# Chunk products of a gated DeltaNet: the triangle mask as a third product in the exponent, beta on ScalarE

## The chip, the cores and the metric

The kernel runs on one core of a Trainium2 chip. The metric is device time in microseconds (us) of one execution, the median of the runs shown. The engines are TensorE (PE in profiles; its weight loads are PEld), VectorE (DVE), ScalarE (ACT), GpSimd (POOL) and SyncE (SP), which issues the transfers. Each works through its own queue in order.

## What is computed

One layer over 2048 latent tokens of width 1024 with 256 context tokens: a neighbourhood attention branch and a bidirectional gated DeltaNet branch, both fed by one projection, merged with gates. The change is in the DeltaNet branch, in the part that is done for every chunk of 64 tokens, head and direction before the scan:

```python
gc = jnp.cumsum(g, axis=-1)
decay = jnp.exp(jnp.where(incl, gc[..., :, None] - gc[..., None, :], -jnp.inf))
kb = k * beta[..., None]
lower = jnp.where(strict, jnp.einsum('bnhid,bnhjd->bnhij', kb, k) * decay, 0.0)
a_mat = lower + jnp.eye(C, dtype=f32)
sol = lax.linalg.triangular_solve(a_mat, rhs, left_side=True, lower=True, unit_diagonal=True)
qk = jnp.einsum('bnhid,bnhjd->bnhij', q, k) * decay
```

C is 64; 36 chunks, 8 heads and 2 directions are computed (the context's chunks without the queries).

## The kernel before

The kernel is one program of stages whose instructions overlap: modulation and normalised, transposed inputs; DeltaNet's k and q with convolution; the chunk products (the stage of the change); DeltaNet's v; the attention's projections and bias tables; then scan and attention together, and the output projections. The program is written in stages, and a scheduler at build time puts each engine's instructions into one fixed order from a timeline that it computes. A change of one stage's instructions so moves others' places too. On the chip each engine takes that order as it stands and waits where an operand isn't there.

The stage of the change is the loop over 18 tiles of two chunks (128 tokens) in `kk_tile`. For a tile, the keys and queries `kq` of both chunks are loaded, and TensorE forms k k^T and q k^T for 8 heads in 32 x 64 pieces (L623) into the accumulator `kk`, which has one buffer. Then, for each of two directions d:

- GpSimd multiplies the log decays, split into a high and a low part (`ghi`, `glo`), with the triangle mask `sm`, 128x512 each (L630, tiles `gmh` and `gml`).
- TensorE adds both up with a triangle of ones, `cmr`, into the accumulator `ps` (pool `pe`, two buffers; L633), which gives the sums of log decays between any two tokens.
- ScalarE takes Exp into E (L635, two buffers).
- GpSimd multiplies E with minus beta (L638) and with the mask (L639).
- VectorE multiplies E with the key products into X (L641) and with the query products in place (L643), both 128x512.
- SP stores X to `d_X` and E to `d_A` (L646, L648). A buffer of E is free for a later Exp when its store has landed.

Between the tiles stands other work, by hand in the program: `pump(fill, ...)` takes 47 gate units, each a product group of 24 products 128x512 (L179) that ScalarE evacuates with Tanh (L205) from one of three accumulators `pd` and SP stores (tile `zt`), with weights that are loaded, cast by ScalarE (L124, tile `slots`) and reduced by GpSimd to their low part (L125). From the third tile on, `solve_for(9000)` hands out steps of the triangular solve by a credit in ns. The solve works on VectorE alone: five blocks (tile `Xs`, one buffer, loaded from `d_X` when the tiles that it holds are stored), each of 62 steps, and step m is two instructions over m x (63 - m) columns, a product (L577) and a sum (L579):

```python
V.tensor_tensor(out=tv, in0=X[r, piv, cols].unsqueeze(1).to_broadcast([8 * n, m, w]),
                in1=X[r, rows, piv].unsqueeze(2).to_broadcast([8 * n, m, w]), op=ALU.mult)
V.tensor_tensor(out=X[r, rows, cols], in0=X[r, rows, cols], in1=tv, op=ALU.add)
```

The first block has 64 rows, the others 128. The solve goes on through the stages behind the loop, where other work on VectorE stands between its steps, and ends before the scan begins. L590 copies the first block's reversed half for its store.

## Time and profile before

| what | us |
|---|---|
| runs, median of 3 | 2428.86 |
| runs, lowest and highest | 2428.39, 2434.27 |
| the profiled execution, its own time | 2437.24 |
| its span | 2435.5 |
| loop over the tiles (first L630 to last L643) | 462.2 to 802.6 |
| first and last step of the solve (L577) | 504.7 to 1408.8 |

A profile shows one execution. Busy time of an engine is the time in which it works on an instruction; a wait is put down to what ended it. Lines L... are those of the kernel before. The chain of work that ended last is followed back from the last instruction, at each step to what released it, and says which work set the end. The granted clock is the share of TensorE's full clock in a stretch.

### The profile page before, as it was taken

What the parts mean: (1) busy time and instruction counts of PE and PEld (TensorE: products, weight loads), DVE (VectorE), ACT (ScalarE), POOL (GpSimd) and SP (SyncE); (2) the same over time, 40 slices, a digit from 0 to 9 for tenths busy, and PEclk for the clock granted to TensorE, in tenths of its full rate; (3) what the DMA queues carried; (4) which work ended last, traced back from release to release, by engine and by line L of the source; (5) the groups of instructions that cost most, each with busy time, mean ns of one, the idle gap of its engine ahead of it and who ended that gap; (6) DMA issues with size and microseconds to landing.
All of it is one profiled execution on the core that took longest, in us unless ns stands there. A gap on an engine that the chain in (4) does not pass through costs nothing.

```text
span 2435.5 us, 47134 instructions
## 1 busy us (share of the span) xinstructions
PE 2208.8 (91%) x18323; PEld 1849.1 (76%) x18323; DVE 1537.0 (63%) x2409; ACT 779.9 (32%) x2336; POOL 1064.2 (44%) x856
## 2 busy tenths in 40 slices
PE   6999999988888998998889987989888989899999
PEld 2778777876676787998888766777666767788998
DVE  3736877379959987849849922666566766222222
ACT  4524344211111232343554111444334444211110
POOL 2515677779865211224857510211123324643442
PEclk8999999998998999999999998999999999999999
DMA  7323444665475244254686567777886786544442
GB/s 262 106 70 81 114 118 130 156 152 121 122 173 134 64 88 115 64 131 119 181 200 176 171 153 205 211 195 196 211 216 178 184 195 177 155 118 121 113 115 89
DMA packets 461591, 358.16 MB, mean 147 GB/s; under 512 B 203253, under 2 KB 386697, under 8 KB 460809
## 3 DMA queue, kind: packets, MB, share of 16 engines
q1 hardware_dynamic: 461368, 355.16, 54.7%
q8 instruction: 144, 2.36, 0.4%
q14 instruction: 79, 0.65, 0.1%
HBM read 231.71 MB, written 119.67 MB: 144 GB/s over the span
## 4 chain that ended last, share of the span: by engine, by line
PE 44%; DVE 20%; DMA 12%; POOL 8%; issue 6%; ACT 4%; SPq 3%; DVEq 0%; POOLq 0%; ACTq 0%
PE pd L179 13%; PE pf L1351 7%; PE pu L1340 7%; DVE Xs L579 6%; DVE tmp L577 6%; PE pd L724 5%; PE pw L1063 2%; DMA tedge<-d_tab 2%; ACT pr L1085 2%; PE pc L866 1%; DMA tmk<-in_k_mk_dram 1%; POOL rn L504 1%; PE po L1116 1%; PE pt L1096 1%; DMA d_tab<-tmk 1%
## 5 line engine op out<-in xcount | busy, mean ns | idle before, releaser
L179 PE MATMUL pd<-hT,slots 128*128 128x512 f32 (+1 forms) x3360 | 825.6, 400 | 4.3 <-ACT nx L205 2.5
L179 PEld LDWEIGHTS pd<-hT,slots 128*128 128x128 f32 x3360 | 627.6, 194 | 152.6 <-issue 3.8
L577 DVE TENSOR_TENSOR tmp<-Xs 128x236 f32<-128x236 f32 (+43 forms) x310 | 337.4, 1088 | 62.4 <-DMA Xs<-d_X 54.1
L579 DVE TENSOR_TENSOR Xs<-Xs,tmp 128x236 f32<-128x236 f32 (+43 forms) x310 | 335.8, 1083 | 8.5
L125 POOL TENSOR_TENSOR slots<-w_raw,slots 128x512 fp32r<-128x512 f32 (+1 forms) x76 | 121.0, 1592 | 252.0 <-ACT slots L124 250.2
L724 PE MATMUL pd<-slots,hT 128*128 128x256 f32 x1248 | 165.5, 293 | 0.0
L724 PE MATMUL pd<-wide,hT 128*128 128x256 f32 x1248 | 158.8, 289 | 3.8 <-ACT wide L124 2.6
L724 PEld LDWEIGHTS pd<-slots,hT 128*128 128x128 f32 x1248 | 159.9, 196 | 0.0
L724 PEld LDWEIGHTS pd<-wide,hT 128*128 128x128 f32 x1248 | 155.7, 195 | 4.5 <-ACT wide L124 3.0
L878 POOL TENSOR_TENSOR sd<-sd,gts 128x512 f32<-128x512 f32 x36 | 37.6, 1045 | 238.4 <-PE pc L866 205.6
L1085 ACT ACTIVATE pr<-pr,nm 128x288 f32<-128x288 f32 (+3 forms) x128 | 77.9, 609 | 165.4 <-DVE nm L1082 165.4
L1341 DVE SCALAR_TENSOR_TENSOR gt<-gt,pu 128x256 f32<-128x256 f32 x120 | 46.3, 418 | 122.2 <-DMA gt<-d_g 76.4
L481 DVE SCALAR_TENSOR_TENSOR y<-raw,vT,y 128x512 f32<-128x512 f32 (+1 forms) x112 | 97.0, 875 | 27.5 <-ACT raw L469 22.0
L777 POOL TENSOR_TENSOR tmk<-trr,tmk 128x288 f32<-128x288 f32 (+3 forms) x72 | 98.7, 1387 | 31.0 <-DMA tmk<-in_k_mk_dram 17.3
L1342 POOL TENSOR_TENSOR gt<-gt 128x256 f32<-128x256 f32 x60 | 44.3, 739 | 127.4 <-DVE gt L1341 126.1
L1355 DVE SCALAR_TENSOR_TENSOR ckd<-pf,gate 128x512 f32<-128x512 f32 x32 | 22.0, 692 | 122.1 <-PE pf L1351 115.3
L689 POOL TENSOR_TENSOR nrn<-nss,nhalf 128x8 f32<-128x8 f32 x34 | 74.0, 2177 | 56.8 <-DVE nss L688 55.1
L205 ACT ACTIVATE zt<-pd 128x512 f32<-128x512 f32 x68 | 40.6, 597 | 180.5 <-PE pd L179 113.2
L1340 PE MATMUL pu<-ckq,OS 128*128 128x256 f32 x512 | 95.2, 284 | 2.1 <-DVE gt L1341 1.3
L124 ACT CAST slots<-w_raw 128x512 fp32r<-128x512 f32 (+1 forms) x76 | 46.6, 613 | 151.1 <-DMA w_raw<-in_w_in_dram 120.2
L866 PE MATMUL pc<-sd,ckq 64*64 64x64 f32 x2176 | 85.0, 232 | 8.5 <-DMA ckq<-d_kq 8.3
L866 PEld LDWEIGHTS pc<-sd,ckq 64*64 64x64 f32 x2176 | 75.0, 144 | 22.3 <-issue 11.3
(295 smaller groups left out, 4589.9 us busy)
## 6 DMA issues: line engine op xcount, KB each, us to landing
w_raw<-in_w_in_dram SPq DMA_DIRECT2D x92, 256.0 KB
ckq<-d_kq SPq DMA_DIRECT2D x64, 256.0 KB
gt<-d_g SPq DMA_DIRECT2D x60, 256.0 KB
d_X<-X SPq DMA_DIRECT2D x72, 128.0 KB
Xs<-d_X SPq DMA_DIRECT2D x18, 512.0 KB
d_g<-zt SPq DMA_DIRECT2D x36, 256.0 KB
cv<-d_v SPq DMA_DIRECT2D x72, 128.0 KB
cT<-d_T SPq DMA_DIRECT2D x72, 128.0 KB
```

Of the source, the lines that this page charges most:

```text
L125: G.tensor_tensor(out=lo[:, j:j + 4, 0:n], in0=wr, in1=hi[:, j:j + 4, 0:n].bitcast(F32), op=ALU.subtract)
L179: PE.matmul(ps[0:n, 0:m], a[:, k, 0:n], h_part(g, z, k), start=k == 0 and i == 0, stop=k == KB - 1 and i == 2)
L481: V.scalar_tensor_tensor(out=y[:, 0:m], in0=raw[:, o + j - 1:o + j - 1 + m], scalar=tap(j), in1=y[:, 0:m], op0=ALU.mult, op1=ALU.add)
L577: V.tensor_tensor(out=tv, in0=X[r, piv, cols].unsqueeze(1).to_broadcast([8 * n, m, w]), in1=X[r, rows, piv].unsqueeze(2).to_broadcast([8 * ...
L579: V.tensor_tensor(out=X[r, rows, cols], in0=X[r, rows, cols], in1=tv, op=ALU.add)
L689: G.tensor_tensor(out=rn, in0=ss, in1=nhalf, op=ALU.pow)
L724: PE.matmul(ps[:, 256 * i:256 * i + 256], h[:, 256 * j + P * i:256 * j + P * i + P], w[:, :, part, k, :], start=k == 0 and n == 0, stop=k ...
L777: G.tensor_tensor(out=mv, in0=rr[:, k0:k0 + nr, w0:w0 + n], in1=mv, op=ALU.add)
L866: PE.matmul(ps[half[d], h, :], ld["ckq"][half[d], ho(h), z, :], sd[half[d], h, :], start=True, stop=True)
L1085: S.activation(e[:, 0:nk], e[:, 0:nk], AF.Exp, bias=nm[:, u:u + 1], accum_out=self.sums[:, hh, 0:1])
L1340: PE.matmul(ps, a, r[:, k, :], start=k == 0 and n == 0, stop=k == 3 and n == 2)
L1351: PE.matmul(ps, a[:, k, P * i:P * i + P], b[k, n], start=k == 0 and m == 0, stop=k == KB - 1 and m == 2)
```

## The change

The triangle mask is taken off E and put into the exponent: `smn` holds -1e30 on the diagonal of each chunk (the product of both directions' masks) and 0 elsewhere. Multiplied with the other direction's triangle `cmr[:, 1 - d]` it gives -1e30 to each pair that is to be masked, so that Exp makes 0 of it. This is a third product per direction on TensorE, first of the three. The product with minus beta moves from GpSimd to ScalarE, as eight instructions 128x64 with a scale per partition. GpSimd keeps the two masked decays, now under one name with three buffers. X had one buffer and keeps it.

```diff
--- before.py
+++ after.py
@@ -340,6 +340,9 @@
     cmr = gp.tile([P, 2, P], F32R, name="cmr")
     sm = gp.tile([P, 2, C], F32, name="sm")
     SP.dma_start(out=sm, in_=k_sm)
+
+    smn = gp.tile([P, C], F32R, name="smn")
+    V.scalar_tensor_tensor(out=smn, in0=sm[:, 0], scalar=BIG, in1=sm[:, 1], op0=ALU.mult, op1=ALU.mult)
     edc = gp.tile([P, 2, NTILE, H], F32, name="edc")
     nbeta = gp.tile([P, 2, NTILE, H], F32, name="nbeta")
     ghi = gp.tile([P, 2, NTILE, H], F32R, name="ghi")
@@ -606,6 +609,8 @@
         pk = st.enter_context(tc.tile_pool(reuse_waits="tile", name="pk", bufs=1, space=PSUM))
         pe = st.enter_context(tc.tile_pool(reuse_waits="tile", name="pe", bufs=2, space=PSUM))
 
+        ho = lambda h: h % 4 * 2 + h // 4
+
         def kk_tile(t):
             main = t >= CT
             n = 2 if main else 1
@@ -625,19 +630,19 @@
                 ps = pe.tile([P, H, C], F32, name="pe")
                 gms = []
                 for nm, g in (("gmh", ghi), ("gml", glo)):
-                    gm = kp.tile([P, 2, 4, C], F32R, name=nm)
+                    gm = kp.tile([P, 2, 4, C], F32R, name="gm", bufs=3)
                     gv = g[:, d, t].bitcast(F32).rearrange("p (q u) -> p u q", u=2).unsqueeze(3).to_broadcast([P, 2, 4, C])
                     G.tensor_tensor(out=gm, in0=gv, in1=sm[:, d].unsqueeze(1).unsqueeze(1).to_broadcast([P, 2, 4, C]), op=ALU.mult)
                     gms.append(gm)
+                PE.matmul(ps, cmr[:, 1 - d, :], smn.unsqueeze(1).to_broadcast([P, H, C]), start=True, stop=False)
                 for i, gm in enumerate(gms):
-                    PE.matmul(ps, cmr[:, d, :], gm.rearrange("p u q e -> p (u q) e"), start=i == 0, stop=i == 1)
+                    PE.matmul(ps, cmr[:, d, :], gm.rearrange("p u q e -> p (u q) e"), start=False, stop=i == 1)
                 E = kp.tile([P, H, C], F32, name="E", bufs=2)
                 S.activation(E, ps, AF.Exp)
-                nb = nbeta[:, d, t].rearrange("p (q u) -> p u q", u=2).unsqueeze(3).to_broadcast([P, 2, 4, C])
+                for h in range(H):
+                    S.mul(E[:, h], E[:, h], nbeta[:, d, t, ho(h):ho(h) + 1])
                 a4 = lambda z: z.rearrange("p (u q) e -> p u q e", u=2)
-                G.tensor_tensor(out=a4(E), in0=a4(E), in1=nb, op=ALU.mult)
-                G.tensor_tensor(out=E, in0=E, in1=sm[:, d].unsqueeze(1).to_broadcast([P, H, C]), op=ALU.mult)
-                X = kp.tile([P, H, C], F32, name="X")
+                X = kp.tile([P, H, C], F32, name="X", bufs=1)
                 V.tensor_tensor(out=a4(X)[:, :, :, ::-1] if d and not main else a4(X), in0=kk[:, :, :, 0:C], in1=a4(E), op=ALU.mult)
                 if main:
                     V.tensor_tensor(out=a4(E), in0=kk[:, :, :, C:2 * C], in1=a4(E), op=ALU.mult)
```

How the new order stands against the old: on GpSimd 72 instructions fewer (L638, L639), on ScalarE 288 more, on TensorE 36 more, on SP as many as before. By the last X of the loop the solve has done 93 steps where it had done 89; the gate products in the loop are 837 where they were 835, counted from the first key product to the last product of decays.

GpSimd in the middle of the loop, before (gmh and gml are the masked decays, slots the weights' low part):

```order
L639 TENSOR_TENSOR E<-E,sm 128x512
L630 TENSOR_TENSOR gml<-glo,sm 128x512
L638 TENSOR_TENSOR E<-E,nbeta 128x512
L639 TENSOR_TENSOR E<-E,sm 128x512
L630 TENSOR_TENSOR gmh<-ghi,sm 128x512
L630 TENSOR_TENSOR gml<-glo,sm 128x512
L125 TENSOR_TENSOR slots<-w_raw,slots 128x512
L638 TENSOR_TENSOR E<-E,nbeta 128x512
```

and in the changed kernel, whose lines stand five to six lower (L635 is the old L630):

```order
L635 TENSOR_TENSOR gm<-ghi,sm 128x512
L635 TENSOR_TENSOR gm<-glo,sm 128x512
L635 TENSOR_TENSOR gm<-ghi,sm 128x512
L635 TENSOR_TENSOR gm<-glo,sm 128x512
L125 TENSOR_TENSOR slots<-w_raw,slots 128x512
L635 TENSOR_TENSOR gm<-ghi,sm 128x512
L635 TENSOR_TENSOR gm<-glo,sm 128x512
```

Only decays and weights are left, and no instruction there waits for ScalarE's Exp any more.

TensorE around the key products of the eighth tile, before:

```order
L633 MATMUL pe<-gmh,cmr 128x512
L179 MATMUL pd<-hT_755,slots 128x512 x2
L179 MATMUL pd<-hT_756,slots 128x512
L623 MATMUL kk<-kq 64x128 x16
L633 MATMUL pe<-gml,cmr 128x512
L179 MATMUL pd<-hT_755,slots 128x512 x2
```

and now (L628 is the old L623; L637 the mask's product; L639 the decays'):

```order
L637 MATMUL pe<-smn,cmr 128x512
L639 MATMUL pe<-gm,cmr 128x512 x2
L179 MATMUL pd<-hT_591,slots 128x512 x2
L179 MATMUL pd<-hT_592,slots 128x512
L179 MATMUL pd<-hT_591,slots 128x512
L628 MATMUL kk<-kq 64x128 x16
L637 MATMUL pe<-smn,cmr 128x512
L639 MATMUL pe<-gm,cmr 128x512 x2
```

The two decay products of a direction, which stood apart with gate products between them in many tiles, now mostly follow each other behind the mask's product.

ScalarE around the seventh tile, before (L635 is Exp, L205 a gate evacuation, L124 a weight cast):

```order
L635 ACTIVATE E<-pe 128x512
L124 CAST slots<-w_raw 128x512
L635 ACTIVATE E<-pe 128x512
L205 ACTIVATE zt<-pd 128x512 x2
L635 ACTIVATE E<-pe 128x512
```

and now (L641 is Exp, L643 the eight products with minus beta):

```order
L641 ACTIVATE E<-pe 128x512
L643 ACTIVATE E<-E,nbeta 128x64 x8
L124 CAST slots<-w_raw 128x512
L641 ACTIVATE E<-pe 128x512
L205 ACTIVATE zt<-pd 128x512
L643 ACTIVATE E<-E,nbeta 128x64 x8
L124 CAST slots<-w_raw 128x512
```

Behind the second Exp an evacuation stands ahead of the eight products. That is so in 8 of the 36 directions; in one a weight cast stands there.

## Rows read from the trace of the kernel before

**Rows 1.** Page, part 1: busy us (share of the span) x instructions of each engine.

```profile
PE 2208.8 (91%) x18323; PEld 1849.1 (76%) x18323; DVE 1537.0 (63%) x2409; ACT 779.9 (32%) x2336; POOL 1064.2 (44%) x856
```

**Rows 2.** Stretches: us, busy of PE, PEld, DVE, ACT, POOL, granted clock, DMA share, GB/s.

```profile
462.00:505.00 43.00, 43.00 (x265) 34.24 (x265) 8.58 (x14) 9.65 (x16) 32.25 (x30) 1.00 0.68 152
505.00:700.00 195.00, 159.70 (x885) 124.58 (x885) 188.30 (x170) 29.75 (x51) 161.49 (x94) 0.91 0.53 126
700.00:735.00 35.00, 30.10 (x155) 23.60 (x151) 10.71 (x20) 4.51 (x8) 18.87 (x17) 0.94 0.93 219
735.00:805.00 70.00, 62.70 (x317) 49.37 (x318) 68.83 (x61) 10.92 (x19) 40.56 (x24) 0.89 0.46 111
805.00:900.00 95.00, 91.62 (x464) 76.10 (x463) 92.84 (x120) 37.43 (x73) 16.09 (x8) 0.98 0.23 64
...
1300.00:1410.00 110.00, 106.19 (x468) 85.40 (x467) 106.53 (x90) 23.00 (x63) 65.57 (x40) 1.00 0.54 161
```

**Rows 3.** Chain that ended last, by line: of 505 to 700, then 1300 to 1410 us.

```profile
by line: DVE Xs L579 27.3%; DVE tmp L577 26.7%; issue 17.3%; PE pd L179 9.9%; DVE E L643 4.6%; DMA d_X<-X 4.1%; DVE X L641 2.1%; PE kk L623 1.7%; DMA w_raw<-in_w_in_dram 1.4%; PE pe L633 1.1%; POOL gmh L630 0.8%; DVE zt L207 0.7%; SPq L646 
...
by line: DVE Xs L579 49.0%; DVE tmp L577 47.0%; SPq L586 2.4%; issue 2.3%; DVE nss L688 1.3%; DVE Xs L581 0.1%
```

**Rows 4.** Stretches, VectorE's L577 alone (two rows), then L579 alone (two rows).

```profile
505.00:700.00 195.00, 81.19 (x61) 0.91 0.53 126
...
735.00:805.00 70.00, 31.17 (x24) 0.89 0.46 111
...
505.00:700.00 195.00, 82.33 (x62) 0.91 0.53 126
...
735.00:805.00 70.00, 30.89 (x24) 0.89 0.46 111
```

**Rows 5.** Groups by form, VectorE, 805 to 1000 us: busy us, mean ns, idle before.

```profile
L577 DVE TENSOR_TENSOR tmp<-Xs 128x980 f32<-128x980 f32 x3 | 3.5, 1179 | 0.1
...
L577 DVE TENSOR_TENSOR tmp<-Xs 128x62 f32<-128x62 f32 x2 | 0.5, 244 | 8.5 <-DMA Xs<-d_X 8.5
```

**Rows 6.** Timeline, VectorE and GpSimd at 617 us: start us, us, instruction.

```profile
617.40 1.91 DVE L579 TENSOR_TENSOR Xs<-Xs,tmp 64x980 f32<-64x980 f32 x1
...
618.24 2.22 POOL L639 TENSOR_TENSOR E<-E,sm 128x512 f32<-128x512 f32 x1
```

**Rows 7.** Lines L630 and L641: duration ns min/median/max, first and last start.

```profile
L630 POOL TENSOR_TENSOR gmh<-ghi,sm x36: 1042/1618/1997, 462.2 to 785.1; 128x512 fp32r<-128x512 f32 x36
...
L641 DVE TENSOR_TENSOR X<-kk,E x36: 671/678/693, 476.4 to 800.9; 128x512 f32<-128x512 f32 x36
```

**Rows 8.** Waits from 505 to 700 us: total us, times, longest.

```profile
ACT zt L205 <- PE pd L179: 53.1, 10, 9.2
...
PE pe L633 <- POOL gmh L630: 17.3, 5, 4.5
...
PE pe L633 <- POOL gml L630: 11.2, 3, 4.3
```

**Rows 9.** Groups, GpSimd, 505 to 700 us: busy us, mean ns, idle before.

```profile
L639 POOL TENSOR_TENSOR E<-E,sm 128x512 f32<-128x512 f32 x20 | 38.9, 1946 | 0.7
...
L638 POOL TENSOR_TENSOR E<-E,nbeta 128x512 f32<-128x512 f32 x21 | 33.9, 1612 | 28.2 <-ACT E L635 28.1
```

**Rows 10.** Timeline, VectorE around 700 to 735 us; idle before, and its releaser, in brackets.

```profile
702.22 0.69 DVE L641 TENSOR_TENSOR X<-kk,E 128x512 f32<-128x512 f32 x1 [3.18 <-POOL E L639]
...
710.20 0.69 DVE L641 TENSOR_TENSOR X<-kk,E 128x512 f32<-128x512 f32 x1 [1.84 <-POOL gmh L630]
...
731.11 0.22 DVE L577 TENSOR_TENSOR tmp<-Xs 128x62 f32<-128x62 f32 x1 [11.66 <-DMA Xs<-d_X]
```

**Rows 11.** Chain that ended last, 455 to 475 us, in order of time: start us, us.

```profile
460.59 9.32 PE pd L179 x40
```

**Rows 12.** Chain, 1230 to 1260 us; then groups of ScalarE over the whole span.

```profile
1248.35 1.75 ACT nx L692 x8
...
L692 ACT ACTIVATE nx<-pd,nrn 128x64 f32<-128x64 f32 x224 | 49.1, 330 | 61.3 <-POOL nrn L689 61.1
```

## The prediction

> **What bounds the kernel now.** The page first: of the span of 2435.5 us TensorE is busy 2208.8, VectorE 1537.0, GpSimd 1064.2 and ScalarE 779.9 [rows 1]. Such shares are means over stages, so the table of stretches comes next [rows 2]. The loop over chunk tiles runs from 462 to about 805 us. Up to 505 us TensorE has no gap at all (43.00 of 43.00). From 505 to 700 us three engines crowd: VectorE 188.30 of 195 us, GpSimd 161.49, and TensorE 159.70 at a granted clock of 0.91, a mean between its levels of 1.2 and 2.4 GHz. From 700 to 735 us VectorE has little to do (10.71), and from 735 to 805 us it is full again (68.83 of 70). The chain of work that ended last, asked for by stretch, says who sets the time: from 505 to 700 us the two lines of the solve, L577 and L579, hold 54%; from 1300 to 1410 us they hold 96% [rows 3]. So the time of the loop is read from VectorE.
>
> Why is VectorE full? From 505 to 700 us it runs nearly all of the first solve block: 61 instructions at L577 and 62 at L579, 81.19 + 82.33 = 163.5 us [rows 4]. The same instructions where GpSimd is nearly idle (805 to 900 us, GpSimd 16.09 of 95 [rows 2]) take 1179 ns for 980 columns and 244 ns for 62 [rows 5]: a line of 181 + 1.019 x columns ns. A block has 62 steps, step m with m x (63 - m) columns, 41,664 in all, and two instructions per step: 2 x (62 x 0.181 + 41,664 x 0.001019) = 107.4 us alone. The excess is 163.5 - 107.4 = 56 us. It goes with GpSimd: at 617 us a step of 980 columns takes 1.91 us and GpSimd's L639 beside it 2.22 [rows 6]; GpSimd's own mask product at L630 is 1.04 us at its least and 1.6 in the middle, while VectorE's product with PSUM, L641, stays between 671 and 693 ns [rows 7]. So an instruction of VectorE with both inputs in SBUF and one of GpSimd slow each other. TensorE, for its part, waits for GpSimd's masked decays at L633, 17.3 + 11.2 = 28.5 us in this stretch [rows 8].
>
> **What the change does, and its prices.**
> 1. It removes L638 and L639, the two products on E: 21 + 20 [rows 9] of GpSimd's 94 instructions of the stretch [rows 2], 36 + 36 in the loop. If the excess of 56 us is shared alike by the 94, these take 41/94 x 56 = 24.4 us with them. Bounds: the 53 that stay can hold VectorE for their own 1.04 us each at most, 55 us, so that only 1 us goes; and at the other end all 56 go. I take the share, since shapes and engine stay the same. **-24.4 us**, on the path, as VectorE sets the end there.
> 2. From 735 to 805 us the solve has 24 + 24 instructions in 31.17 + 30.89 = 62.1 us [rows 4]: steps 6 to 29 of the second block, 17,960 columns, alone 2 x (24 x 0.181 + 17,960 x 0.001019) = 45.3 us by the same line. GpSimd has 24 instructions there [rows 2], some 12 of them the removed kinds (two of each four in the loop). Half of 16.8: **-8.4 us** (between 0 and 16.8).
> 3. From 700 to 735 us VectorE waits twice behind GpSimd, 3.18 us for L639 and 1.84 us behind a masked decay; after these it waits 11.66 us for the load of the next solve block [rows 10]. That transfer is late next. **-3 us** of the 5 (0 to 5).
> 4. It adds 36 products of the mask, 128x512 like those of L179 and L633. 40 of L179 took 9.32 us back to back, 0.233 each [rows 11]: 8.4 us in all. About 8 stand in the first stretch, where TensorE has no gap: 8 x 0.233 = **+1.9 us**. The others fall into the 28.5 us of waiting above; if that cover were gone, the other 28 would cost 6.5 us. A mask product stands first of its three and so waits for the Exp two directions before, which frees the accumulator; behind it on TensorE's queue stand the products of L179. Before, the first decay product had the same wait.
> 5. It adds 288 instructions 128x64 on ScalarE. The nearest row is L692, the same shape with a scale per partition: eight in a row took 1.75 us, 330 ns each when counted singly [rows 12]. So 8 x 0.22 = 1.75 us per direction (bound above 8 x 0.33 = 2.6), 63 us in all. ScalarE is busy 9.65 + 29.75 + 4.51 + 10.92 = 55 of 343 us [rows 2], so there is room; who waits for its queue is rival D. The chain from Exp to X gets shorter: 1.75 us stand where GpSimd took 1.61 + 1.95 [rows 9]. No gain is booked for that beyond point 3. The Trainium skill, "ScalarE: Activation LUTs", Rules for kernel authors, speaks against this step: multiplications belong on VectorE, not on ScalarE. The row speaks against the rule here: one product of 512 columns on VectorE is 0.68 us [rows 7], 36 of them 24 us on the engine that sets the end; by the rule's placement the sum would be about nothing.
> 6. One buffer name with three turns replaces two with one turn each, and smn is one small instruction on VectorE behind the load of sm, beside TensorE's gapless products. Both at nothing: 43.00 of 43.00 us cover them [rows 2]; without that cover smn would cost less than one X, 0.68 us.
> 7. The new order also moves solve steps ahead: by the last X of the loop 93 pairs stand where 89 did. Eight instructions at 62.1/48 = 1.3 us are 10 us more in a stretch that VectorE sets, and as much less later, where the solve sets the end from 1300 to 1410 us. TensorE is nearly full there as well (106.19 of 110 [rows 2]), so I count half as not given back: **+5 us** (0 to 10).
>
> Sum: -24.4 - 8.4 - 3 + 1.9 + 5 = -28.9 us. The profiled execution took 2437.24 us, 1.7 over its span and 8.4 over the median of the three runs, 2428.86. The sum makes 2408 of the one and **2400 us** of the other. What comes after the loop waits for its predecessors, and so moves up as a whole.
>
> **Rivals.**
> B, the collisions vanish: with GpSimd free to run ahead, the remaining decays fall beside VectorE's PSUM products, and all 56 us go. Then TensorE is the limit: its 159.70 us at 0.91 would be 145 at full clock, and 150 with 20 mask products (4.7), a gain of 45 in the stretch. With -16.8, -3, +1.9 and +5 that is -58: 2371 us. For it: TensorE waits for GpSimd so often. Against it: solve steps fill 163.5 of 195 us, so that nearly any GpSimd instruction meets one. Chance 0.10.
> The Trainium skill, "GPSIMD Engine Reference", Key points, says that GpSimd shares its SBUF interfaces with VectorE and contends with instructions that have two SBUF inputs. The trace agrees (1.91 against 1.18 us, and 0.68 undisturbed with one input in PSUM), and by that rule the decays that stay go on colliding, which is against B.
> C, the collisions stay: the 53 remaining instructions lie wholly under solve steps. The stretch gains 1 us, the next one nothing; with -3 and +1.9, and no room to pull steps ahead, the time is 2427 us. For it: GpSimd would merely gain idle time. Chance 0.17.
> D, slower, by ScalarE's queue: the new order has a gate evacuation (L205) between Exp and its eight products in 8 of 36 places, and a weight cast in one. E then waits for a product group of TensorE, and X, the accumulator kk and the next tile's products wait for E. L205 waited 53.1 us in 10 cases in the stretch, 5.3 each [rows 8]. Nine such waits are 48 us; less the 29 gained, +19: 2448 us. It decides from 29/9 = 3.2 us per place on, beyond what is covered. Against it: in most places two to sixteen solve instructions stand on VectorE ahead of the X, and the Exp itself stood behind such evacuations before. Chance 0.08.
> That GpSimd's work doesn't go is excluded: the new order has 72 fewer of its instructions.
>
> **How the numbers follow.** Forecast 0.65, B 0.10, C 0.17, D 0.08. About 0.3%, 7.3 us, is what can be told from no change. Faster by more than that: forecast, B and a little of C, 0.78; within: most of C, 0.14; slower: D, 0.08. The forecast alone, by its terms, has 2383 to 2420. The range goes from 2377, near B, to 2427, at C; outside lie D, half of C and a part of B, about 2 in 10.
>
> **What would show it.** Right: the first block's solve between 125 and 145 us instead of 163.5; GpSimd busy 120 to 150 us less in the loop; no wait of X for E; TensorE's waits for decays nearly gone, its clock above 0.91; the solve still the chain there. B: the solve at 107 to 115 us, and L179 on the chain. C: the solve above 155 us. D: X waiting for ScalarE's products, and these behind L205. The prediction is wrong in another way if the loop gets as short as forecast and the total doesn't follow; then new waits stand between 805 and 1500 us.

## The result and the profile after

| | us |
|---|---|
| before, median of 4 runs beside the changed kernel | 2431.57 (2428.39 to 2438.49) |
| changed kernel, median of 4 runs | 2396.95 (2395.04 to 2401.16) |
| ratio, with its 95% interval | 0.9849 [0.9833, 0.9866] |
| forecast | 2400, range 2377 to 2427 |
| span of the profiled executions | 2435.5 before, 2393.3 after |

The change makes the kernel 1.5% faster: by the ratio 0.0151 x 2431.57 = 36.7 us, by the medians 34.6, where 28.9 were forecast. The spans of the profiled executions differ by 42.2 us, because the kernel before was profiled in an execution above its median (2437.24 us) and the changed one in its fastest (2395.04). Lines are now those of the changed kernel: L635 is the masked decay (before L630), L637 the mask's product, L639 the decay products, L641 Exp, L643 the eight products with minus beta, L646 and L648 VectorE's X and E (before L641 and L643), L580 and L582 the solve (before L577 and L579).

The page, part 1, busy time of each engine:

```profile
PE 2197.7 (92%) x18359; PEld 1842.7 (77%) x18359; DVE 1501.5 (63%) x2410; ACT 850.4 (36%) x2624; POOL 938.6 (39%) x784
```

Against [rows 1]: GpSimd has 72 instructions fewer and 125.6 us less, ScalarE 288 more and 70.5 us more. The line to look at is VectorE: one instruction more, and 35.5 us less busy. No work left VectorE, so its instructions got shorter.

The stretches, in the columns of [rows 2], cut where the first solve block and the loop now end:

```profile
503.00:667.00 164.00, 148.57 (x852) 115.81 (x851) 156.35 (x169) 68.11 (x210) 73.50 (x46) 0.96 0.58 143
667.00:702.00 35.00, 27.62 (x147) 21.68 (x147) 9.76 (x18) 10.04 (x32) 10.35 (x10) 0.96 0.95 219
702.00:777.00 75.00, 72.19 (x397) 57.42 (x394) 73.55 (x75) 26.82 (x79) 23.54 (x14) 0.97 0.53 133
```

In the first stretch VectorE is full as before (156.35 of 164), but this stretch is 31 us shorter than the 195 of [rows 2]; GpSimd works 73.50 us in it where it worked 161.49, and TensorE's clock is 0.96 instead of 0.91. The solve's two lines alone, L580 and then L582:

```profile
503.00:667.00 164.00, 66.63 (x62) 0.96 0.58 143
...
702.00:777.00 75.00, 33.26 (x30) 0.97 0.53 133
...
503.00:667.00 164.00, 66.45 (x62) 0.96 0.58 143
...
702.00:777.00 75.00, 31.99 (x29) 0.97 0.53 133
```

66.63 + 66.45 = 133.1 us for the first block; it was 163.5 [rows 4]. In the 75 us behind the gap the solve now does 30 + 29 instructions where it did 24 + 24 in 70 us.

Why a step is shorter is seen in the timeline of the changed kernel, VectorE first, then GpSimd, and one place a little later:

```profile
605.23 1.88 DVE L580 TENSOR_TENSOR tmp<-Xs 64x950 f32<-64x950 f32 x1
607.04 0.67 DVE L646 TENSOR_TENSOR X<-kk,E 128x512 f32<-128x512 f32 x1
...
612.60 1.84 DVE L580 TENSOR_TENSOR tmp<-Xs 64x920 f32<-64x920 f32 x1
...
604.14 1.97 POOL L635 TENSOR_TENSOR gm<-glo,sm 128x512 fp32r<-128x512 f32 x1
606.07 1.95 POOL L635 TENSOR_TENSOR gm<-ghi,sm 128x512 fp32r<-128x512 f32 x1
...
611.54 1.93 POOL L635 TENSOR_TENSOR gm<-ghi,sm 128x512 fp32r<-128x512 f32 x1
```

GpSimd's products that are left have the same 128x512 shape as those that went, and they still meet the solve: 920 columns take 1.84 us here beside the masked decay of 611.54, and 1.11 us in a kernel below that has no such decay (e7). The product X at 607.04, with one input in PSUM, takes its 0.67 us in the middle of a masked decay. At this place the records read like turns. The decay of 604.14 ends at 606.11, the step of 605.23 ends 1.00 us later, and the next decay, begun at 606.07, ends 0.91 us after that. Each then has, within 0.15 us, the time that it takes alone (a decay 1.045 us at its least, the step about 1.13). The Trainium skill, "SBUF — State Buffer", Who interferes with whom, says the same: a VectorE instruction with two SBUF inputs contends with a GpSimd one that reads SBUF, and the pair of ports goes to one of them for its whole instruction. The trace agrees, the 0.67 us included.

Groups of the loop, 460 to 805 us (busy us, mean ns of one | idle before it and what ended it):

```profile
L643 ACT ACTIVATE E<-E,nbeta 128x64 f32<-128x64 f32 x288 | 72.9, 337 | 0.9
...
L646 DVE TENSOR_TENSOR X<-kk,E 128x512 f32<-128x512 f32 x36 | 24.6, 683 | 28.6 <-ACT slots L124 9.8 <-DMA d_X<-X 9.3 <-PE kk L628 5.7
...
L637 PE MATMUL pe<-smn,cmr 128*128 128x512 f32 x36 | 15.9, 445 | 13.9 <-ACT E L641 13.9
```

ScalarE's products take 72.9 / 288 = 0.253 us each. E was ready at most 2.6 us after the end of its Exp, in all 36 directions. The 9.8 us that the profile puts down to a weight cast are one wait, and not one for ScalarE:

```profile
681.25 2.03 ACT L643 ACTIVATE E<-E,nbeta 128x64 f32<-128x64 f32 x8
...
686.33 0.78 SPq L651 DMA_DIRECT2D d_X<-X  x1
...
694.18 0.69 DVE L646 TENSOR_TENSOR X<-kk,E 128x512 f32<-128x512 f32 x1 [9.78 <-ACT slots L124]
```

The E of this X was done at 683.28 us. X has one buffer, and the instruction waits for the stores of the X before it as well: issued at 684.85 and 686.33 us, their last packets landed at 693.44 and 694.06, and X starts at 694.18. The cast, which ended at 694.15, merely came last by the profile. Waits of the first stretch, 503 to 667 us (total us, times, longest):

```profile
ACT E L641 <- DMA d_A<-E: 52.4, 16, 7.3
...
ACT zt L205 <- PE pd L179: 28.0, 8, 6.3
...
PE pe L637 <- ACT E L641: 13.9, 10, 3.1
...
PE pe L639 <- POOL gm L635: 1.5, 1, 1.5
```

TensorE waited 28.5 us for decays [rows 8]; 1.5 are left. A new wait stands at the mask's product, 13.9 us, for the Exp that frees the accumulator. Exp itself waits 52.4 us for the store that frees E (57.6 us before, from 505 to 700).

How far the whole program moved up, by the timelines of VectorE (us; busy is the solve's two lines):

| solve block | before: start, end, busy | after: start, end, busy | end moved by |
|---|---|---|---|
| 1 | 504.7, 698.3, 163.8 | 503.1, 666.1, 133.1 | -32.2 |
| 2 | 731.1, 898.0, 128.6 | 699.9, 851.8, 120.1 | -46.2 |
| 3 | 926.4, 1059.9, 117.4 | 882.0, 1014.7, 117.2 | -45.2 |
| 4 | 1087.2, 1233.4, 126.5 | 1042.0, 1184.8, 126.2 | -48.6 |
| 5 | 1265.8, 1409.4, 136.9 | 1220.0, 1368.8, 140.0 | -40.6 |

So on VectorE the gain is made by the end of the second block and mostly kept to the end of the solve. It doesn't all reach the scan, the stage behind the solve. TensorE at the scan's first product, before and then after:

```profile
1430.44 2.91 PE L866 MATMUL pc<-sd,ckq 64*64 64x64 f32 x32 [8.30 <-DMA ckq<-d_kq]
```

```profile
1385.49 12.72 PE L179 MATMUL pd<-hT,wide 128*128 128x512 f32 x48 [5.79 <-ACT nx L205]
1398.05 4.36 PE L179 MATMUL pd<-hT,slots 128*128 128x512 f32 x18
1402.35 0.33 PE L871 MATMUL pc<-sd,ckq 64*64 64x64 f32 x2
```

Before, TensorE stood idle for 8.30 us until a load of the scan's operands, and the scan began 21.0 us after the last step of the solve. Now TensorE does 113 products between the two where it did 54, the last 66 of them in the rows above behind a wait of 5.79 us for an evacuation, and the scan begins 33.6 us after the solve. So it starts 28.1 us earlier (1430.4 to 1402.4), not 40.6. The other 14.1 us of the 42.2 come between the scan's first product and the end (1005.0 us before, 990.9 after), where the change edits nothing. The profiles of the twelve kernels below have 994.0 to 1005.8 us there, so this length varies from kernel to kernel by as much as that; the changed kernel's is the shortest of all.

### The profile page after: what moved, and what is told of

It reads as the page before. It is cut to its first block, busy times and chain, and to the rows that moved or that the text cites. A ratio compares the mean times of both kernels' runs of the same rounds, so it can differ in the third digit from the quotient of the medians.

```text
span 2393.3 us, 47334 instructions
## 1 busy us (share of the span) xinstructions
PE 2197.7 (92%) x18359; PEld 1842.7 (77%) x18359; DVE 1501.5 (63%) x2410; ACT 850.4 (36%) x2624; POOL 938.6 (39%) x784
## 5 line engine op out<-in xcount | busy, mean ns | idle before, releaser
L179 PE MATMUL pd<-hT,slots 128*128 128x512 f32 (+1 forms) x3360 | 813.5, 397 | 1.8 <-ACT hT L319 1.7
L179 PEld LDWEIGHTS pd<-hT,slots 128*128 128x128 f32 x3360 | 619.9, 191 | 147.2 <-issue 3.8
L580 DVE TENSOR_TENSOR tmp<-Xs 128x236 f32<-128x236 f32 (+43 forms) x310 | 315.5, 1018 | 38.7 <-DMA Xs<-d_X 25.9
L582 DVE TENSOR_TENSOR Xs<-Xs,tmp 128x236 f32<-128x236 f32 (+43 forms) x310 | 321.1, 1036 | 8.6
L125 POOL TENSOR_TENSOR slots<-w_raw,slots 128x512 fp32r<-128x512 f32 (+1 forms) x76 | 115.7, 1523 | 348.6 <-ACT slots L124 339.4
L782 POOL TENSOR_TENSOR tmk<-trr,tmk 128x288 f32<-128x288 f32 (+3 forms) x72 | 98.0, 1378 | 40.1 <-DMA tmk<-in_k_mk_dram 35.5
L205 ACT ACTIVATE zt<-pd 128x512 f32<-128x512 f32 x68 | 40.4, 594 | 142.8 <-PE pd L179 68.8
L1348 ACT CAST yh<-gt 128x256 fp32r<-128x256 f32 x60 | 24.3, 405 | 187.6 <-POOL gt L1347 187.2
L873 DVE TENSOR_TENSOR cr<-pc,egs 128x512 f32<-128x512 f32 x68 | 46.8, 688 | 66.2 <-DMA cT<-d_T 36.0
L1101 PE MATMUL pt<-ident,pr 128*128 128x128 f32 (+2 forms) x416 | 66.3, 286 | 23.5 <-ACT pr L1090 22.4
```

The lines of the kernel that those rows point to most:

```text
L125: G.tensor_tensor(out=lo[:, j:j + 4, 0:n], in0=wr, in1=hi[:, j:j + 4, 0:n].bitcast(F32), op=ALU.subtract)
L179: PE.matmul(ps[0:n, 0:m], a[:, k, 0:n], h_part(g, z, k), start=k == 0 and i == 0, stop=k == KB - 1 and i == 2)
L782: G.tensor_tensor(out=mv, in0=rr[:, k0:k0 + nr, w0:w0 + n], in1=mv, op=ALU.add)
L1101: PE.transpose(ptw[0:kb, b, :], self.et[u][:, kb * b:kb * b + kb], ident)
```

## The experiments

The theory: the gain is made by the solve's instructions on VectorE, which meet fewer GpSimd instructions. Rivals: the chain from Exp to X, which lost two GpSimd steps; GpSimd's time as such, so that decays come late to TensorE; the buffers. All kernels are edits of the changed one. Kernels were run in three groups, each beside runs of the kernel before, whose median was 2439.98, 2439.51 and 2437.71 us; ratios are to these. The changed kernel ran in none of the three, so it is compared with them by ratios (its own is to 2431.57 us).

### Buffers

```diff
-                    gm = kp.tile([P, 2, 4, C], F32R, name="gm", bufs=3)
+                    gm = kp.tile([P, 2, 4, C], F32R, name="gm", bufs=2)
```

> The changed kernel with two buffers for the masked decays instead of three. Collision theory (VectorE's solve steps and GpSimd's SBUF products slow each other, and the change gains by taking 72 of them off GpSimd): the buffers hardly matter, 2394 to 2406 us, the first solve block's busy time 128 to 140 us. Rival, buffers (GpSimd runs ahead by a third buffer, so that TensorE no longer waits for decays): most of the gain goes, 2415 to 2430 us, with TensorE waiting 20 us or more for decays from 505 to 700 us.

Measured: 2398.98 us, 0.9836 [0.9815, 0.9856]; first block 133.0 us. The third buffer is worth nothing that can be measured. This kernel is the base of the next three.

### GpSimd's instructions put back, off every chain

e1 adds, per direction, two products of GpSimd that nobody reads, of the size that was removed; the work on E stays on ScalarE.

```diff
+                for _ in range(2):
+                    dead = kp.tile([P, H, C], F32, name="dead")
+                    G.tensor_tensor(out=dead, in0=sm[:, d].unsqueeze(1).to_broadcast([P, H, C]), in1=sm[:, 1 - d].unsqueeze(1).to_broadcast([P, H, C]), op=ALU.mult)
```

> The kernel with two buffers, and for each direction two more products 128x512 on GpSimd between constants in SBUF, whose result nobody reads: the removed instructions' traffic without their place in the chain. Collision theory: the first solve block takes 155 to 168 us again and the total is 2418 to 2438 us. Rival, chain (the gain comes from E no longer passing through GpSimd's queue on its way to X): nobody waits for these, so the solve block stays under 142 us and the total is within 8 us of the kernel with two buffers alone.

e2 adds two that keep GpSimd as long, but read only 8 columns (also unread).

```diff
+    half8 = gp.tile([P, 8], F32, name="half8")
+    G.memset(half8, 0.5)
...
+                for _ in range(2):
+                    dead = kp.tile([P, 8], F32, name="dead")
+                    G.tensor_tensor(out=dead, in0=half8, in1=nhalf, op=ALU.pow)
```

> The kernel with two buffers, and for each direction two powers 128x8 on GpSimd that nobody reads: GpSimd is held some 1 to 1.9 us by each, as by the removed products, but with eight columns of SBUF traffic. Collision theory: first solve block 128 to 142 us, total within 8 us of the kernel with two buffers alone. Rival, occupancy (GpSimd's free time is what counts): decays come late, TensorE waits for them over 20 us from 505 to 700 us, total 2415 us or more.

e10 is e2 with `range(1)`, and ran in the third group.

> Two buffers, and one unread power 128x8 per direction on GpSimd in place of two. Held for 1.99 us each it fills GpSimd for 72 us, as the two removed products would if nothing collided with them (72 x 1.04 = 75 us). If only collisions count, within 4 us of the kernel with two buffers alone, a ratio of 0.982 to 0.986; if half of the 17 us that two powers cost goes by GpSimd's time, 0.986 to 0.988.

Measured: e1 2453.56 us, 1.0057 [1.004, 1.0075]; e2 2415.54, 0.9904 [0.9886, 0.9922]; e10 2410.08, 0.9882 [0.9864, 0.99]. The added groups over the whole span, e1 and then e2:

```profile
L647 POOL TENSOR_TENSOR dead<-sm 128x512 f32<-128x512 f32 x72 | 127.8, 1775 | 2.4
```

```profile
L649 POOL TENSOR_TENSOR dead<-half,nhalf 128x8 f32<-128x8 f32 x72 | 143.2, 1989 | 1.5
```

Both hold GpSimd alike, e2 a little longer. Now the stretch of the first solve block, e1 and then e2, in the columns of [rows 2]:

```profile
506.00:718.00 212.00, 162.04 (x856) 123.75 (x856) 201.18 (x166) 69.20 (x213) 193.60 (x111) 0.89 0.47 115
```

```profile
510.00:688.00 178.00, 154.91 (x850) 119.96 (x849) 159.03 (x169) 68.16 (x209) 171.34 (x100) 0.92 0.54 138
```

TensorE, VectorE and ScalarE do nearly the same number of instructions in both. VectorE is busy 201.18 us in the one and 159.03 in the other; the solve's part is 178.6 and 135.8 us. So it is moving 512 columns through SBUF beside the solve that costs, not GpSimd's time: e1 against e2, in one group, is 38 us. (The two kernels differ in what GpSimd reads, in what it writes and in the operation; which of these it is they don't tell apart.) Since e1's products stand on no chain, its time, longer than that of the kernel before, is not the chain's doing; the time from the end of Exp until E is ready is 2.06 us in the median, in e1 as in the changed kernel. Both figures of e1 are above what was expected (155 to 168 and 2418 to 2438 us): the block met 110 large instructions, where the kernel before had 92, and decays came late as well (TensorE waited 39.3 us for them from 506 to 718 us).

The second rival has a smaller share. The solve block of e2 came out as the theory expected, its total as the rival did: e2 is 16.6 us slower than e8. Of its first block, 177.1 us long, the solve leaves 41.3, where it leaves 27.9 in e8 (160.9 - 133.0), 29.9 in the changed kernel (163.0 - 133.1) and 29.8 before. GpSimd is busy 171.34 of 178 us in e2, and decays come late: TensorE's wait for them, 1.5 us in the first stretch of the changed kernel, is in e2, from 510 to 688 us:

```profile
PE pe L641 <- POOL gm L637: 22.4, 14, 3.6
```

In the kernel before, GpSimd was busy 161.49 of 195 us [rows 2], TensorE waited 28.5 us [rows 8], and yet the solve left no more than after the change. So lateness cost the kernel before nothing that shows in the first block (against e8, at most 2 us). With half the added time (e10) the remainder is 170.7 - 139.1 = 31.6 us, and the total is still about 11 us worse than e8's by ratios (0.9882 - 0.9836); part of that is the solve's 139.1 us, as the other order puts 54 large GpSimd instructions beside the first block instead of 51. The ratio is at the upper end of the second expectation, or beyond. By the profiles the scan starts 5.7 us later than in e8, and 4.8 us are lost behind that.

### One half of the change alone

e3 keeps the mask in the exponent and gives beta back to GpSimd.

```diff
-                for h in range(H):
-                    S.mul(E[:, h], E[:, h], nbeta[:, d, t, ho(h):ho(h) + 1])
+                nb = nbeta[:, d, t].rearrange("p (q u) -> p u q", u=2).unsqueeze(3).to_broadcast([P, 2, 4, C])
...
+                G.tensor_tensor(out=a4(E), in0=a4(E), in1=nb, op=ALU.mult)
```

> Only the mask is moved into the exponent; minus beta stays a product on GpSimd, in place on E (36 of the 72 instructions removed). Collision theory: about half of the gain, 2408 to 2420 us, first solve block 143 to 153 us. Chain rival: E still passes through GpSimd, so little of the gain, 2418 us or more, with X waiting for GpSimd.

e4 keeps beta on ScalarE and gives the mask back to GpSimd, without the third product.

```diff
-                PE.matmul(ps, cmr[:, 1 - d, :], smn.unsqueeze(1).to_broadcast([P, H, C]), start=True, stop=False)
...
-                    PE.matmul(ps, cmr[:, d, :], gm.rearrange("p u q e -> p (u q) e"), start=False, stop=i == 1)
+                    PE.matmul(ps, cmr[:, d, :], gm.rearrange("p u q e -> p (u q) e"), start=i == 0, stop=i == 1)
...
+                G.tensor_tensor(out=E, in0=E, in1=sm[:, d].unsqueeze(1).to_broadcast([P, H, C]), op=ALU.mult)
```

> Only minus beta is moved to ScalarE; the mask stays a product on GpSimd, behind ScalarE's eight, and there is no third product on TensorE (36 of the 72 instructions removed). Collision theory: about half of the gain, 2408 to 2420 us, first solve block 143 to 153 us. Chain rival: the way of E is longer than before (Exp, eight products, GpSimd), so 2425 us or more.

Measured: e3 2417.51 us, 0.9912 [0.9892, 0.9932], first block 146.9 us; e4 2418.94, 0.9915 [0.9902, 0.9929], first block 151.3 us. Each half brings 0.9%, together 1.7%, against the whole's 1.5 to 1.6%: they add up, as instructions that each cost the solve a bit would.

### Beta on VectorE

```diff
-                for h in range(H):
-                    S.mul(E[:, h], E[:, h], nbeta[:, d, t, ho(h):ho(h) + 1])
+                nb = nbeta[:, d, t].rearrange("p (q u) -> p u q", u=2).unsqueeze(3).to_broadcast([P, 2, 4, C])
...
+                V.tensor_tensor(out=a4(E), in0=a4(E), in1=nb, op=ALU.mult)
```

> The changed kernel with minus beta as one product 128x512 on VectorE instead of eight on ScalarE. VectorE sets the loop's end: 36 products of 0.7 to 1.1 us are 25 to 40 us more on it, so 2416 to 2434 us, with the solve block itself at 128 to 138 us. Rival (TensorE sets the end by now): within 8 us of the changed kernel.

Measured: 2418.18 us, 0.9909 [0.9895, 0.9923]; slower than the changed kernel by 0.6%, some 15 us. Its product in the loop, 460 to 790 us:

```profile
L644 DVE TENSOR_TENSOR E<-E,nbeta 128x512 f32<-128x512 f32 x36 | 34.2, 954 | 7.3 <-ACT E L641 7.3
```

It takes 954 ns, not the 678 of X [rows 7]: with both inputs in SBUF it meets GpSimd itself. The solve's own time in the first block is near the changed kernel's (136.4 us against 133.1), but the block is longer in all (184.8 against 163.0). By the rule of the Trainium skill, "ScalarE: Activation LUTs", Rules for kernel authors, the multiplication belongs here; the measurement disagrees for a stretch in which VectorE is full, by these 15 us.

### More of it: the decays on ScalarE too

If each remaining GpSimd instruction still costs the solve, moving the decays should bring more. e6 moves the low part, e7 (with 'gmh' in the list as well) both, as eight products 128x64 each.

```diff
-                    G.tensor_tensor(out=gm, in0=gv, in1=sm[:, d].unsqueeze(1).unsqueeze(1).to_broadcast([P, 2, 4, C]), op=ALU.mult)
+                    if nm in ('gml',):
+                        gf = gm.rearrange("p u q e -> p (u q) e")
+                        for h in range(H):
+                            S.mul(gf[:, h], sm[:, d], g[:, d, t, ho(h):ho(h) + 1].bitcast(F32))
+                    else:
+                        G.tensor_tensor(out=gm, in0=gv, in1=sm[:, d].unsqueeze(1).unsqueeze(1).to_broadcast([P, 2, 4, C]), op=ALU.mult)
```

> The changed kernel with the low part's masked decay as eight products 128x64 on ScalarE instead of one on GpSimd: 36 of the 94 SBUF products that GpSimd still has in the loop go. Collision theory carried on: first solve block 118 to 127 us, total 2380 to 2392 us. Rival (TensorE, busy 146.6 of 162 us in the first block's stretch, sets the end): solve block as short, total within 5 us of the changed kernel. Rival (ScalarE's queue): ScalarE gets 70 us more in the loop, and TensorE waits for decays from ScalarE, 2400 us or more.

> Both masked decays on ScalarE: GpSimd keeps only the weights' low parts in the loop. First solve block 108 to 118 us, about what it takes alone. ScalarE has 24 products of 0.25 us and Exp per direction, 6.6 us, 238 us in 36 directions, beside some 60 us of other work, so that it is full in a loop of 310 us: 2395 to 2440 us, with TensorE waiting for ScalarE. If ScalarE's queue did not matter, 2370 to 2385 us.

Measured: e6 2385.4 us, 0.978 [0.9766, 0.9793]; e7 2383.61, 0.9767 [0.9753, 0.9781]. Both beat both kernels, the changed one by about 0.7 and 0.8% by the ratios (0.5 and 0.6% by the medians). Of e7 2395 to 2440 us had been expected, with TensorE waiting for ScalarE; that missed, and the other case, 2370 to 2385, came true. The stretch of the first block, e6, then e7:

```profile
504.00:658.00 154.00, 145.44 (x860) 114.64 (x859) 148.74 (x169) 102.76 (x363) 41.62 (x30) 0.99 0.64 157
```

```profile
510.00:648.00 138.00, 134.07 (x789) 106.23 (x788) 134.39 (x168) 136.00 (x515) 15.29 (x9) 0.99 0.68 164
```

With 9 GpSimd instructions left the block's solve takes 112.2 us, near the 107.4 worked out from steps alone, and TensorE (134.07 of 138), VectorE (134.39) and ScalarE (136.00) are all full. A step in e7, where GpSimd is idle, beside the 1.84 us above:

```profile
603.09 1.11 DVE L580 TENSOR_TENSOR tmp<-Xs 64x920 f32<-64x920 f32 x1
```

Its fifth block ends at 1343.5 us, 25 before the changed kernel's, and its scan starts 25 us earlier too (1377.3), but the program ends only 10 earlier: from the scan's first product to the end e7 takes 1005.8 us, the longest of all the profiles, and the changed kernel 990.9, the shortest. Granted clocks over 100 us lie between 0.91 and 1.00 there and fall differently in each kernel. What takes the time there was not isolated.

### Beta folded into Exp

e13 builds on e6, e12 on e7: Exp becomes eight instructions 128x64 with the logarithm of beta as bias, which makes the product with beta superfluous; the sign goes into VectorE's products.

```diff
-        V.tensor_scalar(out=nbeta, in0=beta, scalar1=-1.0, scalar2=None, op0=ALU.mult)
+        S.activation(nbeta, beta, AF.Ln)
...
-                S.activation(E, ps, AF.Exp)
...
-                    S.mul(E[:, h], E[:, h], nbeta[:, d, t, ho(h):ho(h) + 1])
+                    S.activation(E[:, h], ps[:, h], AF.Exp, bias=nbeta[:, d, t, ho(h):ho(h) + 1])
```

> Both masked decays on ScalarE and beta's product folded into Exp: eight Exp 128x64 per direction with the logarithm of beta as bias, and the sign in VectorE's two products. ScalarE, busy 136.0 of 138 us in the first block's stretch without this, is relieved of one instruction of 0.6 us per direction and GpSimd stays empty. If ScalarE held that kernel back, 2368 to 2380 us, ratio 0.970 to 0.975; if what follows the loop sets the end, 2380 to 2390 us, ratio 0.975 to 0.979.

> The same folding with only the low part's decay on ScalarE. ScalarE has room there already (102.8 of 154 us), so no gain is expected over that kernel without the folding: ratio 0.975 to 0.981. If the shorter chain from the accumulator to X counts, 0.970 to 0.975.

Measured: e12 2379.29 us, 0.9764 [0.9746, 0.9781]; e13 2380.87, 0.9767 [0.9752, 0.9783]. Less ScalarE work brings nothing clear beyond e7 and e6 (the intervals overlap), so ScalarE's queue isn't what holds e7 back: in e12 it is busy 125.75 of 140 us (506 to 646), where it was 136.00 of 138, and the first block is no shorter (139.7 us against 137.0). These four are the fastest kernels measured, and alike.

### The mask's product twice

```diff
                 PE.matmul(ps, cmr[:, 1 - d, :], smn.unsqueeze(1).to_broadcast([P, H, C]), start=True, stop=False)
+                PE.matmul(ps, cmr[:, 1 - d, :], smn.unsqueeze(1).to_broadcast([P, H, C]), start=False, stop=False)
```

It adds the -1e30 a second time.

> The changed kernel with the mask's product on TensorE made twice (the masked places get -2e30 in place of -1e30, and Exp still gives 0): 36 more products at 0.233 us each back to back. Cover theory (TensorE has gaps in the loop, so that such a product costs only where there are none): 0 to 4 us over the changed kernel, a ratio to before of 0.984 to 0.988. Rival (TensorE sets the loop by now, busy 146.6 of 162 us in the first block's stretch): the full 8.4 us or more, a ratio of 0.988 to 0.992.

Measured: 2415.37 us, 0.9906 [0.989, 0.9922]: 0.57%, some 14 us, above the changed kernel. The rival's range holds, the cover theory's doesn't. The last X stands at 781 us where it stood at 773. That is about 36 x 0.233 = 8.4 us [rows 11], but the solve has done 97 steps by then instead of 93, so the last X alone doesn't tell TensorE's products from VectorE's steps. The solve itself is not later (first block to 664.6 us, fifth to 1363.1, 5.6 us before the changed kernel's). TensorE is. The stretch behind the last X of the changed kernel, e9's row:

```profile
777.00:860.00 83.00, 83.00 (x413) 68.83 (x412) 72.79 (x99) 27.49 (x52) 8.93 (x6) 1.00 0.38 86
```

TensorE has no gap there. Between the solve's end and the scan's first product it does 167 products where it did 113 in the changed kernel; the last 96 + 18 follow a wait like the one there, which had 48 + 18 behind it:

```profile
1383.39 23.54 PE L179 MATMUL pd<-hT,wide 128*128 128x512 f32 x96 [7.24 <-ACT nx L205]
...
1411.32 0.75 PE L872 MATMUL pc<-sd,ckq 64*64 64x64 f32 x6 [0.19 <-DMA ckq<-d_kq]
```

The scan starts 8.9 us later (1411.3 against 1402.4) although the solve ends earlier: so TensorE's queue holds it, and the delay is about the products' own time. The remaining 5.8 us of the span come behind that (996.7 us against 990.9), within what the kernels vary by there.

### All runs together

GpSimd's 128x512 instructions between the first and last step of the first block, the solve's busy time, and (busy - 107.4) per instruction:

| kernel | GpSimd | solve, us | excess each, us |
|---|---|---|---|
| e1 | 110 | 178.6 | 0.65 |
| before | 92 | 163.8 | 0.61 |
| e4 | 69 | 151.3 | 0.64 |
| e3 | 68 | 146.9 | 0.58 |
| e10 (and 20 small) | 54 | 139.1 | 0.59 |
| e5 | 52 | 136.4 | 0.56 |
| e8 | 51 | 133.0 | 0.50 |
| e2 (and 50 small) | 50 | 135.8 | 0.57 |
| e9 | 48 | 135.9 | 0.59 |
| after | 45 | 133.1 | 0.57 |
| e6 | 30 | 124.9 | 0.58 |
| e13 | 29 | 121.1 | 0.47 |
| e7 | 9 | 112.2 | 0.53 |
| e12 | 8 | 109.8 | 0.30 |

From 29 to 110 instructions the first block's solve loses 0.47 to 0.65 us for each, whichever product it is. With 8 or 9 the excess, 2.4 and 4.8 us, is too small beside the 107.4 us, which are worked out and not measured. Without the 107.4, e1 against e7 gives (178.6 - 112.2) / (110 - 9) = 0.66 us each.

## Why the prediction was right

1. **E's products off GpSimd** (-24.4): right, and a little small. The first block is 30.6 us shorter (193.6 to 163.0), all of it the solve's (163.8 to 133.1). The share by count holds, as the last table shows; the count was short, because 92 instructions became 45 and not 53. Neither bound, 1 or 56 us, was near.
2. **The second stretch** (-8.4): right. The second block's solve went from 128.6 to 120.1 us, -8.6.
3. **The gap** (-3): failed. From the end of block 1 to the start of block 2 it is 33.8 us where it was 32.8. The load of the block is late next, as said, but it comes no earlier after the last step of block 1: the two waits had not delayed it. One of them was also misread: the 1.84 us put down to a masked decay were the store of X, whose last packets landed at 710.08 us, ahead of the X of 710.20 (a masked decay is no operand of X). Such a store holds X for 9.78 us in the changed kernel's gap, at 694.18 us above; it is not rival D's wait. The load of the second block was issued by 688.69 us and landed at 699.79, and the block's first step follows, though its row names another load:

```profile
699.87 0.22 DVE L580 TENSOR_TENSOR tmp<-Xs 128x62 f32<-128x62 f32 x1 [4.27 <-DMA kq<-d_kq]
```

4. **The mask's products** (+1.9): too small. "The others fall into the 28.5 us of waiting" is the sentence that failed. That waiting went with GpSimd's work (1.5 us left), and the mask's product brought a wait of its own (13.9 us for Exp; the prediction said that the first decay product had the same wait before, but from 505 to 700 us of the kernel before no product of L633 waits for Exp). By e9, 36 such products cost 8 to 9 us at the scan's start rather than 1.9. The changed kernel's scan waits for TensorE's queue too, so most of its own 8.4 us should stand there; that is inferred from e9, not measured.
5. **ScalarE's products** (0.22 each, hidden): 0.253 each, within the two bounds, and hidden. The loop has room for 288 more (e6) and, less clearly, for 576 (e7). Against the rule of the Trainium skill the row was right in sign; the rule's placement loses 15 us and not the 24 worked out from [rows 7], although each product took 954 ns. That the rest fell into VectorE's waits is likely, and not shown.
6. **Buffers and smn** (nothing): right by e8.
7. **Steps ahead** (+5): failed. On VectorE the 4 pairs ahead and what moved with them cost nothing in the end. Behind the loop, from its last X to the end of block 2, 97 us became 79: 35 + 35 solve instructions became 31 + 31 (66.5 to 56.0 us), and of the next stage's work on VectorE 46 instructions became 34. Rows of before (802 to 898 us), then after (774 to 852 us):

```profile
L579 DVE TENSOR_TENSOR Xs<-Xs,tmp 128x980 f32<-128x980 f32 (+30 forms) x35 | 35.2, 1005 | 0.6
...
L481 DVE SCALAR_TENSOR_TENSOR y<-raw,vT,y 128x512 f32<-128x512 f32 (+1 forms) x31 | 23.9, 778 | 0.5 <-ACT y L471 0.5
```

```profile
L582 DVE TENSOR_TENSOR Xs<-Xs,tmp 128x992 f32<-128x992 f32 (+30 forms) x31 | 29.5, 953 | 0.7
...
L484 DVE SCALAR_TENSOR_TENSOR y<-raw,vT,y 128x512 f32<-128x512 f32 (+1 forms) x23 | 16.1, 719 | 0.0
```

The 12 instructions are given back later: of the second block's 15.0 us (166.9 to 151.9) 8.6 are shorter steps and 6.4 other work that moved behind, and from the second to the fifth block's end the lead falls by 5.6 us. So the sum is, by the ends of blocks: -1.6 (an earlier start) - 30.6 + 1.0 - 8.6 - 6.4 + 5.6 = -40.6 us at the end of the solve. Against the -28.9 of the forecast that is 11.7 us more: 6.2 from step 1, 0.2 from step 2, 5.8 from step 7 (-0.8 instead of +5), 1.9 from step 4, which doesn't show in the blocks, and 1.6 from the earlier start, less the 4 of step 3.

"What comes after the loop waits for its predecessors, and so moves up as a whole" is another sentence that failed. Of the 40.6 us 12.6 are lost between the solve's end and the scan's first product (21.0 us became 33.6), where TensorE's queue (113 products, and the wait of 5.79 us among them) and no longer the solve alone holds the scan. That leaves 28.1 us at the scan's start, nearly the forecast, and so near it partly by luck: VectorE gained 11.7 us more than forecast, and TensorE, whose terms were too small, took 12.6 back. The 14.1 us behind the scan's start have no term in the forecast and no cause shown; 7.6 of the 42.2 us are the choice of the executions, by their distance from the medians. The mechanism, fewer collisions of the solve with GpSimd, is what the runs show. That the medians moved by 34.6 us, 5.7 beyond the forecast, is not shown to be its doing.

The range that the prediction gives the forecast alone, 2383 to 2420 us, doesn't come out of the bounds of its terms, which are wider.

The signs that were named: the first block between 125 and 145 us (133.1); GpSimd 120 to 150 us less (125.6 over the span); TensorE's waits for decays nearly gone (1.5); the clock above 0.91 (0.96); X waits for ScalarE's products once, 3.7 us at 476 us, before the solve begins. That the solve still sets the end is read from VectorE, 156.35 of 164 us; the chain that ended last can't be followed through that stretch in the profile after. Rival B would have been e7's block (112.2 us), which takes five times fewer GpSimd instructions than the change leaves. Rival C would have had the block above 155 us.

## What to carry to other kernels

Where VectorE with both inputs in SBUF sets the time, count GpSimd's instructions that move tiles through SBUF beside it and price each by a share of its own time alone (here 0.6 of 1.04 us); a row of a product with one input in PSUM is the undisturbed check. An engine with room, here ScalarE, with eight small instructions, is then worth more than a cheaper instruction on the bound engine. And before a wait is used as cover for new work, ask whether the same change takes the wait away. Then look at the next stage's first instruction on each engine: what one engine gains counts there only as far as the others have come too.

## What the runs showed that was not expected

The loss per GpSimd instruction depends little on how busy GpSimd is: 0.58 us in e6 with 41.62 of 154 us busy, 0.65 in e1 with 193.60 of 212. A `pow` of 128x8 on GpSimd takes 1989 ns, longer than a 128x512 product that meets the solve (1775), and the solve hardly feels it: with 50 of them beside the first block it takes 135.8 us, and 133.0 in e8 without them. TensorE's granted clock over the first block, a mean between its two levels, differs as well: it is 0.89 in e1, 0.91 before, 0.92 in e2, 0.96 after and 0.99 in e6 and e7, with TensorE busy 162.04 of 212, 159.70 of 195, 154.91 of 178, 148.57 of 164, 145.44 of 154 and 134.07 of 138 us.
